# Attention probabilities turned in 32x32 blocks on VectorE and moved between partition quadrants by DMA, in a two-layer encoder trunk

## The chip, the cores and the metric

The kernel runs on one core of a Trainium2 chip. The metric is device time in microseconds, the median of several executions. A core has a matrix engine (TensorE, PE in the profile, with its weight loads as PEld), VectorE (DVE), ScalarE (ACT), GpSimd (POOL), and SyncE (SP), whose queue here issues nearly all DMAs. The on-chip memory SBUF has 128 partitions; a quadrant is 32 of them. Matmuls write to PSUM, which is divided into banks.

## The reference

Two identical layers over a sequence of 256 positions with 1024 channels, in float32. Each layer is a half-step SwiGLU block, a mixer and another half-step SwiGLU block. The mixer is where the change is:

```python
h = rms_norm(x, norm_mix[l])
proj = h @ w_in[l]                       # q, k, v, u, g: 512 columns each
q, k, v, u, g = jnp.split(proj, splits, axis=-1)
a = dilated_attention(partial_rotary(heads(q)), partial_rotary(heads(k)), heads(v))   # 8 heads x 64
sg = gelu(u) * (w_s @ layer_norm(gelu(g)) + b_s)                                      # 4 groups x 128
mixed = concatenate([rms_norm(a, out_norm_attn[l]), rms_norm(sg, out_norm_sgu[l])])
x = x + mixed @ w_out[l]
```

The three dilated softmaxes of the attention, merged by their denominators, are computed as one softmax over 256 keys with an additive bias table. The output is the final RMSNorm of x.

## The kernel before, in words

Positions lie on partitions: `NT = 2` tiles of 128. Every product with a weight matrix is made of three matmuls of 512 columns: weights and activations are split into a high part (`hi`, type fp32r) and a remainder (`lo`), and `multiply` (L150) adds hi x hi, hi x lo and lo x hi for each block of 128 rows `k` and each position tile `t`. One call of `multiply` uses one *unit* of the weight stream, 4 blocks of 128 x 512, so 24 matmuls. Before its matmuls, `run_ahead` (L139) writes down the next work of the stream: the load of a unit up to five ahead (`load_unit`, one DMA of 1 MB on SP into one of 3 `raw` buffers, L119) and the split of the unit two ahead (`split_unit`: on ScalarE the high part `whi`, L133; on VectorE the remainder `wlo`, L134; 3 buffers each). A load waits for the split that frees its `raw` buffer. The argument `among` of `multiply` names functions that are called ahead of block `j`, so that other work is written between the matmuls.

The order in which the program is written is not the order in each engine's queue. A planner takes the written order as priority and, with its own estimates of how long each instruction takes, puts on each engine the first instruction that it believes ready. The queues are fixed when the program is built, and each engine then works through its own in order.

The mixer (`mixer`, L511) goes through the units q, k, v, g, u and then four units of `w_out`. The attention is done in two groups of four heads (`a` = 0, 1):

- `scores(a, t)` makes q times k in PSUM, and a VectorE instruction (L571) adds the bias table and takes the row maximum; `softmax(a, t)` takes exponentials on ScalarE (L580) and scales by the reciprocal sum on VectorE (L583). The result `pr[a]` has queries on partitions. `attend(0)` and `attend(1)` are written into the two g units.
- `turn_probs(a)` turns `pr[a]` so that keys lie on partitions: 16 transposes of 128x128 on TensorE (L596) into PSUM tiles `pt`, copied to `prT[a]` half by VectorE (L598), half by ScalarE (L600). It is written into the first u unit for group 0 and at the start of the second for group 1.
- `values(a)` multiplies `prT[a]` by v (tile `pav`, L627, 16 matmuls of 256 columns) and evacuates to `aT` (L632 on ScalarE, L633 on VectorE) and to its squares `sq` (L635). It is written ahead of blocks 1 and 3 of the second u unit.
- `normalise` takes Gelu and layer norm of g to `vv` (L649 to L658). `gate` multiplies `vv` by the spatial weights (tile `mixed`, L690) and by `uu`, the Gelu of u (L678), to `sg`; `turn_sg` transposes that to `sgT`.
- The output projection takes `aT` (accumulators `oa`, two of them, `d` = 0, 1) and then `sgT` (accumulators `os`). `square_sums` (tile `ss`, L673) and `inverse_root` give the norm's factor, and `add` (L705) adds an accumulator to x with it.

Accumulators come from a PSUM pool of four banks, two for each of `g`, `u`, `oa` and `os`; a bank is free again when its last reader is done: `normalise` for g, `uu` for u, `add` for `oa`. Another pool of four banks holds `sc`, `pt`, `pav`, `mixed` and `ss`. Tiles with the same tag (`h0` to `h5`) share one SBUF buffer in turn.

Of the kernel before, what the change touches and what calls it, by code (L numbers as in the profile page):

```python
# [10 lines left out]
F32 = mybir.dt.float32  # L11
F32R = mybir.dt.float32r
BF16 = mybir.dt.bfloat16
AF = mybir.ActivationFunctionType
ALU = mybir.AluOpType
PSUM = bass.MemoryType.PSUM

P = 128
D = 1024
S = 256  # L20
NT = S // P
DEPTH = 2
H = 8
DH = 64
DA = 512
# [62 lines left out]
def trunk_kernel(ctx: ExitStack, tc: tile.TileContext, ws, x, cxt, rows, sgw, ident, bias, rot, out):  # L88
    nc = tc.nc
# [3 lines left out]
    big = ctx.enter_context(tc.tile_pool(name="big", bufs=1))  # L93
# [3 lines left out]
    ps_sc = ctx.enter_context(tc.tile_pool(name="ps_sc", bufs=4, space=PSUM))  # L97
# [52 lines left out]
    def multiply(acc, lhs, start, stop, among={}):  # L150


        i = done["used"]
        done["used"] += 1
        run_ahead(i + 1)
        hi, lo = splits.pop(i)
        ks = UNITS[i][2]
        for j, k in enumerate(ks):
            if j in among:
                among[j]()  # L160
            xh, xl = lhs(k)
            wh, wl = hi[:, j * W:(j + 1) * W], lo[:, j * W:(j + 1) * W]
            for t in range(NT):
                s = slice(t * P, (t + 1) * P)
                nc.tensor.matmul(acc[t], xh[:, s], wh, start=start and j == 0, stop=False)  # L165
                nc.tensor.matmul(acc[t], xh[:, s], wl, start=False, stop=False)  # L166
                nc.tensor.matmul(acc[t], xl[:, s], wh, start=False, stop=stop and j == len(ks) - 1)  # L167
# [35 lines left out]
    def accumulators(name, pool=None, tag="acc"):  # L203
        return [(pool or ps_acc).tile([P, W], F32, tag=tag, name=f"{name}{t}") for t in range(NT)]
# [54 lines left out]
    def inverse_root(ssq, n):  # L259

        v = small.tile([P, 3, NT], F32, tag="root", name="root")
        if ssq.shape[2] == 2:
            nc.gpsimd.tensor_tensor(v[:, 0], ssq[:, :, 0], ssq[:, :, 1], op=ALU.add)
            src = v[:, 0]
        else:
            src = ssq[:, :, 0]
        nc.gpsimd.tensor_scalar(v[:, 1], src, 1.0 / n, EPS, op0=ALU.mult, op1=ALU.add)
        nc.gpsimd.tensor_tensor(v[:, 2], v[:, 1], half.to_broadcast([P, NT]), op=ALU.pow)
        return v[:, 2]
# [241 lines left out]
    def mixer(l, st, nxt):  # L511
# [28 lines left out]


        pr = [big.tile([P, NT, 4, S], F32, tag=f"h{2 + a}", name="pr") for a in range(2)]
        prT = [big.tile([P, 4, 2, S], F32, tag="h4", name="prT")]
        mx = small.tile([P, NT, 2, H], F32, tag="mx", name="mx")
        sm = small.tile([P, NT, 2, H], F32, tag="sm", name="sm")

# [39 lines left out]
        def attend(a):  # L586
            for t in range(NT):
                scores(a, t)
                softmax(a, t)

        def turn_probs(a):
            for h in range(4):
                pt = ps_sc.tile([P, 2, S], F32, tag="sc", name="pt")
                for kt in range(2):
                    for t in range(NT):
                        nc.tensor.transpose(pt[:, kt, t * P:(t + 1) * P], pr[a][:, t, h, kt * P:(kt + 1) * P], id_sb)  # L596
                if h % 2:
                    nc.vector.tensor_copy(prT[a][:, h], pt)  # L598
                else:
                    nc.scalar.activation(prT[a][:, h], pt, AF.Copy)  # L600

        multiply(accs[0], st.lhs, False, True)
        rotate(0, r8)
# [8 lines left out]

        acc_g = accumulators("g")
        multiply(acc_g, st.lhs, True, False, {2: lambda: attend(0)})
        multiply(acc_g, st.lhs, False, True, {1: lambda: attend(1)})


        aT = big.tile([P, 2, 4, S], F32R, tag="h1", name="aT")
# [2 lines left out]
        def values(a):  # L621
            bank = ps_sc.tile([P, 2, S], F32, tag="sc", name="pav")
            for p in range(2):
                for kt in range(2):
                    for j in range(2):
                        h = 2 * p + j
                        nc.tensor.matmul(bank[j * DH:(j + 1) * DH, p], vs[:, kt, (4 * a + h) * DH:(4 * a + h + 1) * DH],  # L627
                                         prT[a][:, h, kt], start=kt == 0, stop=kt == 1)
            for p in range(2):
                k = 2 * a + p  # L630
                g = col(l, 24 + k)
                nc.scalar.activation(aT[:, 0, k], bank[:, p], AF.Copy, scale=g)  # L632
                nc.vector.scalar_tensor_tensor(aT[:, 1, k], bank[:, p], g, f32(aT[:, 0, k]),  # L633
                                               op0=ALU.mult, op1=ALU.subtract)
            nc.scalar.activation(sq[:, 2 * a:2 * a + 2], bank, AF.Square)  # L635


        acc = accumulators("u")
        prT.append(big.tile([P, 4, 2, S], F32, tag="h0", name="prT"))
        multiply(acc, st.lhs, True, False, {1: lambda: turn_probs(0)})  # L640
        vv = big.tile([P, NT, W], F32, tag="vv", name="vv")

        def normalise():

            vn = [act.tile([P, W], F32, tag="s", name="vn") for _ in range(NT)]
            st6 = small.tile([P, NT, 6], F32, tag="st6", name="st6")
            mv = small.tile([P, NT, 2], F32, tag="mv", name="mv")
            for t in range(NT):
                tc.keep_in_program_order(nc.scalar.activation(vn[t], acc_g[t], AF.Gelu, scale=r[:, t:t + 1]))  # L649
                nc.vector.bn_stats(st6[:, t], vn[t])  # L650
                nc.vector.bn_aggr(mv[:, t], st6[:, t])
            rs = small.tile([P, 2, NT], F32, tag="rs", name="rs")
            nc.gpsimd.tensor_scalar(rs[:, 0], mv[:, :, 1], 1.0, EPS, op0=ALU.mult, op1=ALU.add)
            nc.gpsimd.tensor_tensor(rs[:, 1], rs[:, 0], half.to_broadcast([P, NT]), op=ALU.pow)
            for t in range(NT):
                nc.vector.scalar_tensor_tensor(vn[t], vn[t], mv[:, t, 0:1], ln_sb[:, l, 0],
                                               op0=ALU.subtract, op1=ALU.mult)
                nc.vector.scalar_tensor_tensor(vv[:, t], vn[t], rs[:, 1, t:t + 1], ln_sb[:, l, 1],  # L658
                                               op0=ALU.mult, op1=ALU.add)

        def values_and_gate():
            values(0)
            normalise()

        multiply(acc, st.lhs, False, True, {0: lambda: turn_probs(1), 1: values_and_gate, 3: lambda: values(1)})
        nc.vector.tensor_tensor(sq[:, :2], sq[:, :2], sq[:, 2:], op=ALU.add)
        nc.vector.tensor_tensor(sq[:, 0], sq[:, 0], sq[:, 1], op=ALU.add)
        ssq_a = small.tile([P, NT, 1], F32, tag="ssq_a", name="ssq_a")

        def square_sums():  # L670
            bank = ps_sc.tile([P, NT, 1], F32, tag="sc", name="ss")
            for t in range(NT):
                nc.tensor.matmul(bank[:, t], sq[:, 0, t * P:(t + 1) * P], ones, start=True, stop=True)  # L673
            nc.vector.tensor_copy(ssq_a, bank)
# [4 lines left out]


        sg = big.tile([P, NT, W], F32, tag="sg", name="sg")
        sgT = big.tile([P, 2, 4, S], F32R, tag="h2", name="sgT")
        ssq_s = small.tile([P, NT, 1], F32, tag="ssq_s", name="ssq_s")

        def gate():
            for g0 in (0, 2):
                bank = ps_sc.tile([P, 2, NT, P], F32, tag="sc", name="mixed")
                for g in range(2):
                    s = slice((g0 + g) * P, (g0 + g + 1) * P)
                    nc.tensor.matmul(bank[:, g], sgw_sb[:, l, g0 + g, :], vv[:, :, s], start=True, stop=True)  # L690
                for g in range(2):
                    s = slice((g0 + g) * P, (g0 + g + 1) * P)
                    nc.vector.scalar_tensor_tensor(sg[:, :, s], bank[:, g], col(l, 32 + g0 + g), uu[:, :, s],
                                                   op0=ALU.add, op1=ALU.mult)
            for t in range(NT):
                square_sum(ssq_s[:, t], sg[:, t])
# [5 lines left out]
        def add(acc, d, rt):  # L702
            for t in range(NT):
                xs = x_sb[:, t, d * W:(d + 1) * W]
                nc.vector.scalar_tensor_tensor(xs, acc[t], rt[:, t:t + 1], xs, op0=ALU.mult, op1=ALU.add)  # L705
# [4 lines left out]
        def a_lhs(k):  # L710
            return aT[:, 0, k], aT[:, 1, k]

        for d in (0, 1):
            acc = accumulators("oa")
            multiply(acc, a_lhs, True, True, {1: gate, 3: square_sums} if d == 0 else {0: turn_sg})
            if d == 0:
                r_a = inverse_root(ssq_a, DA)
            add(acc, d, r_a)
        r_s = inverse_root(ssq_s, DG)
        new = nxt()  # L720
        for d in (0, 1):
# [97 lines left out]
```

## Time and profile before

| what | value |
|---|---|
| median of 3 runs | 920.57 us (920.27 to 920.67) |
| profiled execution | 922.07 us, span 920.3 us |
| busy: PE / PEld / DVE / ACT / POOL | 912.4 / 750.2 / 751.1 / 466.3 / 21.5 us |
| granted TensorE clock | 0.999 |
| DMA | 174.14 MB, mean 189 GB/s |

The span is the time from the first to the last instruction of one profiled execution. Busy time is the time in which an engine had an instruction in work. A row of instruction groups gives line, engine and operation, output and inputs, shape and count, then busy time, mean ns of one, and idle time of the engine just before. A timeline row gives start, length, engine, line and operation, and in brackets the idle time before it and what ended it. A row of time windows gives the window, its length and then each engine's busy time in the order PE, PEld, DVE, ACT, POOL with the number of instructions, the clock, the DMA share and GB/s. The first mixer's units g to `os` lie between about 221 and 281 us, the second layer's 453 us later.

### The profile page before, as it was taken

Reading aid. Unit: us, or ns where it says so; the run is one execution under the profiler, and the core shown is the slowest. Engines: PE = TensorE matmul, PEld = TensorE weight load, DVE = VectorE, ACT = ScalarE, POOL = GpSimd, SP = SyncE. Lnnn points to the kernel's source line nnn. Section 1 sums busy time; section 2 is a strip of 40 time slices with the busy share of each in tenths; the row PEclk is TensorE's granted clock in tenths of the full one; section 3 lists DMA queues with packets and bytes.
Section 4 is the critical chain, followed back from the end, with each engine's and each line's share of the span. In section 5 each row is a group of like instructions: output and inputs, shape, how many; then the busy total and the mean of one; then the engine's idle time right before and its main releaser. Section 6 shows DMA issues by size and latency. Waiting matters only on the chain.

```text
span 920.3 us, 11062 instructions
## 1 busy us (share of the span) xinstructions
PE 912.4 (99%) x4178; PEld 750.2 (82%) x4178; DVE 751.1 (82%) x1203; ACT 466.3 (51%) x654; POOL 21.5 (2%) x48
## 2 busy tenths in 40 slices
PE   9999999999999999999999999999999999999997
PEld 6888888888778888888888888888887888888886
DVE  6698996796789699896687998966887887998854
ACT  6544544356756544434445544445467545444440
POOL 0000000000010000000000000000000100000000
PEclk9999999999999999999999999999999999999999
DMA  8765555565334645646555555455543455565351
GB/s 330 297 259 183 187 201 205 187 217 192 138 113 175 215 141 206 219 147 237 192 197 177 192 213 191 152 209 208 201 140 135 164 202 183 183 210 200 126 195 47
DMA packets 26982, 174.14 MB, mean 189 GB/s; under 512 B 3120, under 2 KB 4272, under 8 KB 6960
## 3 DMA queue, kind: packets, MB, share of 16 engines
q1 hardware_dynamic: 26496, 172.86, 52.6%
q8 instruction: 33, 0.54, 0.2%
q10 hardware_dynamic: 432, 0.56, 0.2%
q14 instruction: 21, 0.17, 0.1%
HBM read 172.36 MB, written 1.05 MB: 188 GB/s over the span
## 4 chain that ended last, share of the span: by engine, by line
PE 97%; DVE 1%; issue 1%; ACT 0%; DMA 0%; POOL 0%; POOLq 0%; DVEq 0%
PE down L165 8%; PE down L166 8%; PE down L167 8%; PE gate L166 7%; PE up L166 7%; PE up L167 7%; PE gate L167 7%; PE up L165 7%; PE gate L165 7%; PE both L166 2%; PE both L165 2%; PE both L167 2%; PE g L165 1%; PE q L167 1%; PE g L166 1%; PE os L165 1%
## 5 line engine op out<-in xcount | busy, mean ns | idle before, releaser
L134 DVE TENSOR_TENSOR wlo<-raw,whi 128x1024 fp32r<-128x1024 f32 (+2 forms) x325 | 378.4, 1201 | 105.1 <-ACT whi L133 102.8
L133 ACT ACTIVATE whi<-raw 128x1024 fp32r<-128x1024 f32 (+2 forms) x325 | 322.4, 1039 | 246.9 <-issue 100.1
L276 DVE STREAM_TRANSPOSE turned<-h 32x256 f32<-32x256 f32 (+1 forms) x384 | 158.9, 414 | 6.3
L167 PE MATMUL down<-whi,hT 128*128 128x512 f32 x340 | 132.3, 389 | 0.0
L165 PE MATMUL down<-whi,hT 128*128 128x512 f32 x340 | 132.3, 389 | 0.0
L166 PE MATMUL down<-wlo,hT 128*128 128x512 f32 x340 | 132.3, 389 | 0.0
L167 PE MATMUL gate<-whi,xTl 128*128 128x512 f32 x304 | 118.3, 389 | 0.0
L167 PE MATMUL up<-whi,xTl 128*128 128x512 f32 x304 | 118.3, 389 | 0.0
L166 PE MATMUL gate<-wlo,xTh 128*128 128x512 f32 x304 | 118.3, 389 | 0.0
L165 PE MATMUL up<-whi,xTh 128*128 128x512 f32 x304 | 118.3, 389 | 0.0
L166 PE MATMUL up<-wlo,xTh 128*128 128x512 f32 x304 | 118.3, 389 | 0.0
L165 PE MATMUL gate<-whi,xTh 128*128 128x512 f32 x304 | 118.1, 389 | 0.0
L167 PEld LDWEIGHTS down<-whi,hT 128*128 128x128 f32 x340 | 63.8, 188 | 13.3
L165 PEld LDWEIGHTS down<-whi,hT 128*128 128x128 f32 x340 | 63.8, 188 | 13.3
L166 PEld LDWEIGHTS down<-wlo,hT 128*128 128x128 f32 x340 | 63.8, 188 | 13.2
L279 ACT ACTIVATE hT<-turned 128x512 fp32r<-128x512 f32 x44 | 26.8, 626 | 80.2 <-DVE turned L276 80.2
L165 PEld LDWEIGHTS gate<-whi,xTh 128*128 128x128 f32 x304 | 57.1, 188 | 11.9
L165 PEld LDWEIGHTS up<-whi,xTh 128*128 128x128 f32 x304 | 57.1, 188 | 11.9
L166 PEld LDWEIGHTS up<-wlo,xTh 128*128 128x128 f32 x304 | 57.1, 188 | 11.9
L166 PEld LDWEIGHTS gate<-wlo,xTh 128*128 128x128 f32 x304 | 57.1, 188 | 11.9
L167 PEld LDWEIGHTS up<-whi,xTl 128*128 128x128 f32 x304 | 57.1, 188 | 11.8
L167 PEld LDWEIGHTS gate<-whi,xTl 128*128 128x128 f32 x304 | 57.0, 188 | 11.8
(172 smaller groups left out, 1064.7 us busy)
## 6 DMA issues: line engine op xcount, KB each, us to landing
raw<-in_ws SPq DMA_DIRECT2D x154, 1024.0 KB, 4.8
raw<-in_ws SPq DMA_DIRECT2D x8, 512.0 KB, 3.2
raw<-in_ws SPq DMA_DIRECT2D x7, 256.0 KB, 5.5
x_sb<-in_x SPq DMA_DIRECT2D x1, 1024.0 KB, 10.8
ln_sb<-in_rows SPq DMA_DIRECT2D x1, 1024.0 KB, 7.4
out<-y SPq DMA_DIRECT2D x2, 320.0 KB, 2.5
xt_sb<-in_cxt SPq DMA_DIRECT2D x1, 512.0 KB, 7.9
sgw_sb<-in_sgw SPq DMA_DIRECT2D x1, 512.0 KB, 6.5
```

What stands on the lines that cost most here:

```text
L133: nc.scalar.activation(hi[:, s], raw[:, s], AF.Copy)
L134: nc.vector.tensor_tensor(lo[:, s], raw[:, s], f32(hi[:, s]), op=ALU.subtract)
L165: nc.tensor.matmul(acc[t], xh[:, s], wh, start=start and j == 0, stop=False)
L166: nc.tensor.matmul(acc[t], xh[:, s], wl, start=False, stop=False)
L167: nc.tensor.matmul(acc[t], xl[:, s], wh, start=False, stop=stop and j == len(ks) - 1)
L276: nc.vector.transpose(to[32 * c:32 * c + 32, :, :, b, :], frm[32 * b:32 * b + 32, :, :, c, :])
L279: nc.scalar.activation(dst_hi, src, AF.Copy)
```

## The change

`turn_probs(a)` no longer uses TensorE or PSUM. Two VectorE transposes (one per position tile) turn each 32x32 block of `pr[a]` within its own quadrant and write to `tmp`; then 16 DMAs on SP move each quadrant's blocks (32 partitions x 2 KB) to the quadrant they belong to, in `dst`, which takes over the buffer of `pr[a]`. `values` reads `dst` through a pattern of runs of 32 elements. The calls are written at other places: `turn_probs(0)` right after the first g unit, `turn_probs(1)` after the second, `normalise` ahead of the second u unit, `values(0)` ahead of the last block of that unit, and `values(1)` with `gate` ahead of block 2 of the first `oa` unit. Both `oa` accumulators are opened together; the square sums, `turn_sg` and the first `add` are written into the second `oa` unit. `sgT` moves from buffer `h2` to `h5`.

```diff
-        prT = [big.tile([P, 4, 2, S], F32, tag="h4", name="prT")]
+        prT = []
...
         def turn_probs(a):
-            for h in range(4):
-                pt = ps_sc.tile([P, 2, S], F32, tag="sc", name="pt")
-                for kt in range(2):
-                    for t in range(NT):
-                        nc.tensor.transpose(pt[:, kt, t * P:(t + 1) * P], pr[a][:, t, h, kt * P:(kt + 1) * P], id_sb)
-                if h % 2:
-                    nc.vector.tensor_copy(prT[a][:, h], pt)
-                else:
-                    nc.scalar.activation(prT[a][:, h], pt, AF.Copy)
+            tmp = big.tile([P, 4, 16, 32], F32, tag=("h4", "h0")[a], name="prB")
+            for t in range(NT):
+                nc.vector.transpose(tmp[:, :, 8 * t:8 * t + 8].rearrange("p c q j -> p q c j"),
+                                    pr[a][:, t].rearrange("p h (k c i) -> p (h k) c i", c=4, i=32))
+            dst = big.tile([P, 4, 16, 32], F32, tag=("h2", "h3")[a], name="prT")
+            for b in range(4):
+                for c in range(4):
+                    nc.sync.dma_start(dst[32 * c:32 * c + 32, b], tmp[32 * b:32 * b + 32, c])
+            prT.append(dst)
...
         multiply(acc_g, st.lhs, True, False, {2: lambda: attend(0)})
+        turn_probs(0)
         multiply(acc_g, st.lhs, False, True, {1: lambda: attend(1)})
+        turn_probs(1)
...
-                        nc.tensor.matmul(bank[j * DH:(j + 1) * DH, p], vs[:, kt, (4 * a + h) * DH:(4 * a + h + 1) * DH],
-                                         prT[a][:, h, kt], start=kt == 0, stop=kt == 1)
+                        probs = prT[a].rearrange("p b (t q) j -> p q t b j", t=NT)[:, 2 * h + kt]
+                        nc.tensor.matmul(bank[j * DH:(j + 1) * DH, p].rearrange("p (t b j) -> p t b j", t=NT, b=4),
+                                         vs[:, kt, (4 * a + h) * DH:(4 * a + h + 1) * DH], probs,
+                                         start=kt == 0, stop=kt == 1)
...
-        prT.append(big.tile([P, 4, 2, S], F32, tag="h0", name="prT"))
-        multiply(acc, st.lhs, True, False, {1: lambda: turn_probs(0)})
+        multiply(acc, st.lhs, True, False)
...
-        def values_and_gate():
-            values(0)
-            normalise()
-
-        multiply(acc, st.lhs, False, True, {0: lambda: turn_probs(1), 1: values_and_gate, 3: lambda: values(1)})
-        nc.vector.tensor_tensor(sq[:, :2], sq[:, :2], sq[:, 2:], op=ALU.add)
-        nc.vector.tensor_tensor(sq[:, 0], sq[:, 0], sq[:, 1], op=ALU.add)
+        normalise()
+        multiply(acc, st.lhs, False, True, {3: lambda: values(0)})
...
         def square_sums():
+            nc.vector.tensor_tensor(sq[:, :2], sq[:, :2], sq[:, 2:], op=ALU.add)
+            nc.vector.tensor_tensor(sq[:, 0], sq[:, 0], sq[:, 1], op=ALU.add)
...
-        sgT = big.tile([P, 2, 4, S], F32R, tag="h2", name="sgT")
+        sgT = big.tile([P, 2, 4, S], F32R, tag="h5", name="sgT")
...
-        for d in (0, 1):
-            acc = accumulators("oa")
-            multiply(acc, a_lhs, True, True, {1: gate, 3: square_sums} if d == 0 else {0: turn_sg})
-            if d == 0:
-                r_a = inverse_root(ssq_a, DA)
-            add(acc, d, r_a)
+        def values_and_gate():
+            values(1)
+            gate()
+
+        accs = [accumulators("oa") for _ in range(2)]
+        multiply(accs[0], a_lhs, True, True, {2: values_and_gate})
+
+        def add_first():
+            add(accs[0], 0, r_a[0])
+
+        r_a = []
+
+        def root_first():
+            square_sums()
+            r_a.append(inverse_root(ssq_a, DA))
+
+        multiply(accs[1], a_lhs, True, True, {0: root_first, 1: turn_sg, 3: add_first})
+        add(accs[1], 1, r_a[0])
```

## The prediction

> **What bounds the kernel now.** I read the page's head, its busy totals and the chain that ended last first, because they say which engine the end belongs to.
>
> ```profile
> span 920.3 us, 11062 instructions
> ...
> PE 912.4 (99%) x4178; PEld 750.2 (82%) x4178; DVE 751.1 (82%) x1203; ACT 466.3 (51%) x654; POOL 21.5 (2%) x48
> ...
> PE 97%; DVE 1%; issue 1%; ACT 0%; DMA 0%; POOL 0%; POOLq 0%; DVEq 0%
> ```
>
> TensorE (PE) carries 97% of the chain: a microsecond taken off its queue is a microsecond of span, until something else is late. VectorE (DVE) is next, at 82%, and it is VectorE that gets more work here. The profiled execution took 922.07 us with a span of 920.3 us; the median of the three runs is 920.57 us. I form differences on the span and take them off the median.
>
> Next I read the chain in order of time where the transposes stand (start, length).
>
> ```profile
> 237.53 0.23 PE u L167
> 237.76 1.75 PE pt L596 x16
> 239.50 0.23 PE u L165
> ...
> 246.72 1.88 PE pav L627 x16
> ...
> 703.77 0.60 ACT sq L635
> 704.37 1.28 ACT L649
> ...
> 710.76 0.76 DVE vv L658
> 711.52 0.14 issue
> 711.65 1.96 PE mixed L690 x8
> ```
>
> Sixteen transposes cost 1.75 us between two u matmuls. There are four such groups (two head groups, two layers). In the second layer the chain leaves PE and runs through ScalarE's (ACT's) Gelu to vv: even now the side work ends just as PE needs it, so the mixer has little slack.
>
> **The change, part by part.** The groups that are removed or serve as a measure:
>
> ```profile
> L596 PE MATMUL pt<-id_sb,pr 128*128 128x128 f32 x64 | 7.6, 272 | 0.0
> L598 DVE COPY prT<-pt 128x512 f32<-128x512 f32 x8 | 5.3, 681 | 0.0
> L600 ACT ACTIVATE prT<-pt 128x512 f32<-128x512 f32 x8 | 4.2, 580 | 0.0
> L583 DVE TENSOR_TENSOR pr<-pr,sm 128x1024 f32<-128x1024 f32 x8 | 9.8, 1224 | 0.2
> L276 DVE STREAM_TRANSPOSE turned<-h 32x256 f32<-32x256 f32 x320 | 139.6, 436 | 5.2
> L276 DVE STREAM_TRANSPOSE turned<-h 32x128 f32<-32x128 f32 x64 | 19.4, 303 | 1.1
> ```
>
> *Removed.* 64 transposes: 4 x 1.75 = 7.0 us off PE, 3.5 per layer, all of it on the chain. Eight copies of 0.68 us leave VectorE and eight of 0.58 us leave ScalarE.
>
> *Added on VectorE.* Eight transposes of 128x1024. No such shape is in the trace. The two shapes that are differ by 128 elements and 133 ns, so 1.04 ns an element, and 303 - 133 = 170 ns is fixed: 170 + 1024 x 1.04 = 1.24 us if all four quadrants run side by side. The low end is that; the high end, quadrants one after another, is four times it, 4.9 us. I take 1.24, next to the 1.22 us of the 128x1024 multiply on all partitions. Net on VectorE per layer: 4 x 1.24 - 4 x 0.68 = +2.2 us.
>
> *Added on SP.* 16 copies per head group of 32 partitions x 2 KB (64 KB), 64 in all, on the queue that issues the weight loads.
>
> ```profile
> 31.25 0.43 SPq L223 DMA_DIRECT2D rot_sb<-in_rot  x1
> 31.73 0.42 SPq L223 DMA_DIRECT2D bias_sb<-in_bias  x1
> ```
> ```profile
> raw<-in_ws SPq DMA_DIRECT2D x154, 1024.0 KB, 4.8
> ...
> out<-y SPq DMA_DIRECT2D x2, 320.0 KB, 2.5
> ...
> rot_sb<-in_rot SPq DMA_DIRECT2D x1, 32.0 KB, 4.7
> ```
> ```profile
> SPq L119 <- DVE wlo L134: 74.3, 12, 13.5
> ```
>
> Issues follow at 0.48 us (31.25 to 31.73), so 16 take 7.7 us. No row shows a copy inside SBUF. For the landing I take the 2.5 us of the output store, which leaves SBUF on an idle queue; the ends are 0.4 us (the issue alone) and 4.7 us (behind loads). From the last transpose to usable probabilities it is thus 7.2 + 2.5, say 9.7 us, between 7.6 and 12. The Trainium skill, "DMA: Bandwidth & Descriptors", section "Anatomy of one DMA", gives about 2.0 us fixed plus bytes over 436 GB/s, an estimate of 2.15 us for 64 KB on a path other than this one; by it the time would be about 9.4 us. No row of this trace shows such a copy.
>
> *What waits behind them on SP.* The loads. In the 90 us around the first mixer (200 to 290) SP sat 74.3 us waiting for splits, so it has the time. A load that left at 245 us now leaves at about 254 and lands at 259 (4.8 us); its split stands at 263.2 in the trace, about 260 to 261 now. I cost this at nothing; if a landing took over 7 us the splits would slip by the rest.
>
> *The consumers are moved later* (first layer's clock).
>
> ```profile
> 236.23 0.39 PE L165 MATMUL u<-whi,xTh 128*128 128x512 f32 x1
> 236.46 0.39 PE L166 MATMUL u<-wlo,xTh 128*128 128x512 f32 x1
> ...
> 269.34 0.39 PE L165 MATMUL os<-whi,sgT 128*128 128x512 f32 x1
> ```
> ```profile
> 232.51 1.22 DVE L583 TENSOR_TENSOR pr<-pr,sm 128x1024 f32<-128x1024 f32 x1
> ...
> 240.11 1.28 DVE L598 COPY prT<-pt 128x512 f32<-128x512 f32 x2
> ...
> 241.51 1.22 DVE L583 TENSOR_TENSOR pr<-pr,sm 128x1024 f32<-128x1024 f32 x1
> ```
>
> A matmul takes 0.227 us, a unit of 24 takes 5.45. Without transposes PE is at values(0), before the last 6 of u's 48, at 236.2 + 9.5 = 245.7. Head group 0 is scaled at 233.7; its transposes end at 235 to 236 and its copies have landed by about 246. No wait, or a few tenths.
>
> values(1) is the tight one. Head group 1 is scaled at 242.7 in the trace; ahead of that VectorE gets two transposes (2.4) and loses two copies (1.3), and its own last transpose follows (1.2): about 245 to 246.5. Plus 9.7: usable at 256. PE gets to values(1) in source order at 249.0 (u ends, with values(0)'s 1.88) + 12 x 0.227 = 251.7. That is over 4 us early. The trace shows that queues are not in source order: mixed, written behind 6 oa matmuls, ran at 258.54 behind 15, when vv was there. With the first 12 matmuls of the second oa (2.7) and mixed (1.96) put ahead of it, PE arrives at 256.4, and the wait is covered. This is what I take.
>
> *What is late next.* Three things, all on VectorE and ScalarE.
>
> ```profile
> 248.65 0.47 ACT L632 ACTIVATE aT<-pav,cols_sb 128x256 fp32r<-128x256 f32 x1 [1.98 <-PE pav L627]
> ...
> 250.70 0.60 ACT L635 ACTIVATE sq<-pav 128x512 f32<-128x512 f32 x1 [0.55 <-DVE aT L633]
> ...
> 254.35 1.38 ACT L678 ACTIVATE uu<-u,root 128x512 f32<-128x512 f32 x2
> ```
> ```profile
> 263.76 0.19 POOL L267 TENSOR_SCALAR root<-ssq_a 128x2 f32<-128x2 f32 x1 [6.77 <-DVE ssq_a L674]
> 264.04 0.69 POOL L268 TENSOR_TENSOR root<-root,half 128x2 f32<-128x2 f32 x1
> ```
> ```profile
> 233.64:269.34 35.70, 35.56 (x194) 28.09 (x192) 29.42 (x53) 23.39 (x47) 4.86 (x8) 1.00 0.34 120
> ```
>
> First, the second oa's accumulators are u's banks, free only after uu (1.38 us), which on ScalarE queues behind values(0)'s evacuation (248.65 to 251.30, 2.65 us): ready at about 252, wanted at 251.7; I take 0.5 us. Second, mixed needs vv, which now starts right behind the last exponentials; I take 0.6 us. Third, os needs the first oa's banks, so add_first, so root_a, so both head groups' squares: 258.3 (values(1) ends) + 2.65 + about 1.0 for two square sums + 0.4 + 0.9 on POOL + 1.4 for add_first = 264.7 if nothing is ahead of any step, against 265.8 when PE wants it (269.3 - 3.5). But VectorE (fourth number of the row) was busy 29.4 of these 35.7 us; with +2.2, and one split (2.35) deferred past os, it is 29.3 of 32.2, 91% where it was 82%. A step then often finds an operation of 1.2 us ahead of it; three entries on VectorE, so I take 1.5 us.
>
> Waits of 0.5 + 0.6 + 1.5 = 2.6 us against 3.5 saved: 0.9 us a layer, 1.8 in all. 920.6 - 1.8 = 918.8 us.
>
> *Small items.* The values matmuls read and write 32-element runs instead of rows of 256: I take 1.88 us as now; the high end is double, 7.5 us in all. Normalise moves ahead of the second u unit, which feeds vv earlier; the table loads stay two per layer. The square sums and the sgT buffer only change place.
>
> **The rivals.**
>
> *B, nothing is late.* Copies issue faster than I take (0.33 us is the shortest issue on SP) and VectorE's idle time soaks up the rest: the whole 7.0 us, 913.6, range 912.5 to 916.5. For it: 6.3 us of VectorE idle in the row above. Against it: the second layer's chain through vv.
>
> *C, values(1) stands at its source place on PE.* The queue order is fixed ahead of the run; if the planner takes a copy for cheap, PE is at values(1) at 251.7 to 254 and stands until 256: 2.5 to 6 us of idle per layer, and everything behind it that needed values(1) starts no sooner. It decides from 3.5 us of wait on. With 4.5 to 5.5 us plus 0.5 of the other waits it gives 1.5 to 2.5 us lost per layer: 923.6 to 925.6, call it 924. This is the case on the other side.
>
> *C2, the same with a slow clock behind it.* The start shows what PE does before it has been busy:
>
> ```profile
> 8.58 0.63 PE L181 MATMUL up<-wlo,xTh 128*128 128x512 f32 x1
> 9.01 0.63 PE L182 MATMUL up<-whi,xTl 128*128 128x512 f32 x1
> ...
> 10.07 0.39 PE L182 MATMUL up<-whi,xTl 128*128 128x512 f32 x1
> 10.30 0.39 PE L180 MATMUL gate<-whi,xTh 128*128 128x512 f32 x1
> ```
>
> The matmuls start 0.43 us apart up to 9.4 us and 0.23 apart from then on. If each wait of C brings back some ten matmuls at that pace, 10 x 0.2 = 2 us more per layer: 928. The Trainium skill, "TensorE: Matmul & The Clock Gate", section "Why this matters for your kernels", says to leave no idle gaps above about 3 us between bursts, else the clock drops to half. The trace has no idle gap of PE of that length to try this on; the change of pace at the start agrees with a gate that opens with work.
>
> *D, transposes are dear.* At 4.9 us each VectorE gets 14.8 us more per layer than I took; less the 6.3 idle, and with splits then late for PE, 8 to 12 us lost per layer: 935 to 945.
>
> **How the numbers follow.** This kernel's runs agree within 0.04%, and 0.2% (1.84 us) is about what can be told from no change. Forecast 0.43, own range 916.5 to 920.8 (waits of 1.5 to 3.6 us per layer): half of it faster, half the same. B 0.14, faster. C 0.18 and C2 0.15, slower but for 0.01. D 0.06, slower. Left 0.04, no change. So faster 0.36, same 0.25, slower 0.39. The range leaves out B's best half, the upper half of C2 and D: 913.8 to 928.0. The predicted time is the likeliest case's, 918.8.
>
> **What would show it.** No pt group of L596's kind and 3.5 us less PE work per mixer: the first term. A DVE STREAM_TRANSPOSE of 128x1024 x8: 1.2 us, or D. The SP queue's 16 issues in 7 to 8 us; from the last transpose to the first pav matmul of head group 1 about 10 us. PE's idle before pav in the waits: under 1 us per layer says forecast, 3 us or more says C, with matmuls 0.43 us apart behind it C2. Idle before the second oa, mixed and os: my 0.5, 0.6 and 1.5. The prediction is wrong if the planner's order on PE keeps values(1) ahead of the second oa, or if the copies land in much less than 9 us.

## The result, and the profile after

The changed kernel takes 928.48 us (median of 4 runs, 927.73 to 929.88) against 920.53 us for the kernel before beside it: a ratio of 1.0088, 95% interval 1.0071 to 1.0106. It is 8 us slower, where 918.8 was forecast, and half a microsecond beyond the range of 913.8 to 928.0. The profiled execution took 928.1 us.

The head of its page, the busy totals, the chain, the DMA issues of the copies (count, size, median us to landing) and one group of instructions (last column: idle time of the engine just before):

```profile
span 926.3 us, 10997 instructions
...
PE 908.1 (98%) x4114; PEld 744.9 (80%) x4114; DVE 755.3 (82%) x1203; ACT 462.7 (50%) x646; POOL 21.4 (2%) x48
...
PE 92%; DVE 6%; issue 1%; POOL 1%; DMA 0%; POOLq 0%; ACT 0%; DVEq 0%
...
prT<-prB SPq DMA_DIRECT2D x64, 64.0 KB, 2.0
```
```profile
L596 DVE STREAM_TRANSPOSE prB<-pr 128x1024 f32<-128x1024 f32 x8 | 9.9, 1240 | 0.1
```

PE's busy time fell by 4.3 us, not 7.0, and VectorE (DVE) now holds 6% of the chain. To see where, I divided the span at the mixers. Time windows from the first g matmul to the first gate matmul of the next block, first of the kernel before, then of the changed one (columns: window, length, busy time of PE, PEld, DVE, ACT and POOL, clock, DMA):

```profile
221.56:281.14 59.58, 59.44 (x335) 47.55 (x334) 49.08 (x96) 40.29 (x83) 5.25 (x10) 1.00 0.36 133
674.62:734.23 59.61, 59.43 (x336) 47.56 (x334) 49.10 (x96) 40.30 (x83) 5.24 (x10) 1.00 0.37 132
```
```profile
219.96:283.37 63.41, 58.45 (x304) 45.83 (x303) 51.19 (x96) 38.48 (x79) 5.19 (x10) 0.97 0.48 158
676.85:740.26 63.41, 58.44 (x304) 45.56 (x302) 51.19 (x96) 38.47 (x79) 5.18 (x10) 0.97 0.49 158
```

Each mixer is 3.8 us longer, 7.6 in all; between the mixers (393.48 us in both) and behind the second (186.0) nothing changed. The two profiled executions reached the first mixer 1.6 us apart, so I compare these stretches and not the spans. 3.5 us less PE work a mixer and 3.8 us more time means that 7.3 us a mixer were lost. PE busy is 1 us less, since some of the loss is slow matmuls: the clock is 0.97 here.

What PE waited for (us in total, times, longest):

```profile
PE oa L167 <- DVE aT L639: 5.3, 2, 2.7
PE os L167 <- DVE sgT L293: 1.8, 2, 0.9
...
PE oa L165 <- ACT aT L638: 1.1, 2, 0.6
...
PE pav L632 <- DMA prT<-prB: 0.8, 1, 0.8
```

The longest is not the wait for the copies but the one behind it, for `aT`. (In the second layer PE stood 0.8 us ahead of `pav` too; the view puts that down to VectorE, so the row for the copies counts one.) PE's timeline there, in the first layer:

```profile
245.29 0.39 PE L167 MATMUL u<-whi,xTl 128*128 128x512 f32 x1
246.44 1.95 PE L632 MATMUL pav<-prT,v 128*64 128x256 f32 x16 [0.76 <-DMA prT<-prB]
248.95 0.50 PE L165 MATMUL oa<-whi,aT 128*128 128x512 f32 x1 [0.56 <-ACT aT L638]
...
249.75 0.40 PE L166 MATMUL oa<-wlo,aT 128*128 128x512 f32 x1
252.85 1.05 PE L167 MATMUL oa<-whi,aT 128*128 128x512 f32 x2 [2.70 <-DVE aT L639]
253.69 0.63 PE L165 MATMUL oa<-whi,aT 128*128 128x512 f32 x1
254.12 0.63 PE L166 MATMUL oa<-wlo,aT 128*128 128x512 f32 x1
...
255.83 0.63 PE L167 MATMUL oa<-whi,aT 128*128 128x512 f32 x1
256.25 0.50 PE L165 MATMUL oa<-whi,aT 128*128 128x512 f32 x1
256.60 0.39 PE L166 MATMUL oa<-wlo,aT 128*128 128x512 f32 x1
...
259.25 1.95 PE L632 MATMUL pav<-prT,v 128*64 128x256 f32 x16
...
271.26 0.49 PE L167 MATMUL os<-whi,sgT 128*128 128x512 f32 x1 [0.87 <-DVE sgT L293]
```

PE had 0.8 us of idle before pav, 0.6 before the first oa matmuls, did four of them, and then stood 2.7 us. Behind that, eight matmuls follow each other 0.42 to 0.43 us apart instead of 0.23: 1.6 us. Near os (idle 0.87 and the gaps on both sides of it) 1.7 us are lost. That is 0.9 + 0.6 + 2.9 + 1.6 + 1.7 = 7.7 us with the switching around each wait counted in, less 0.4 of the same kind before: the 7.3 us.

`aT` of group 0 needs its high part (ScalarE) and its remainder (VectorE). VectorE's timeline and SP's issues:

```profile
249.19 0.75 DVE L663 SCALAR_TENSOR_TENSOR vv<-vn,rs,ln_sb 128x512 f32<-128x512 f32 x1 [0.86 <-POOL rs L659]
249.86 0.75 DVE L661 SCALAR_TENSOR_TENSOR vn<-vn,mv,ln_sb 128x512 f32<-128x512 f32 x1
250.52 1.22 DVE L134 TENSOR_TENSOR wlo<-raw,whi 128x1024 fp32r<-128x1024 f32 x1
251.65 0.74 DVE L663 SCALAR_TENSOR_TENSOR vv<-vn,rs,ln_sb 128x512 f32<-128x512 f32 x1
252.32 0.48 DVE L639 SCALAR_TENSOR_TENSOR aT<-pav,cols_sb,aT 128x256 fp32r<-128x256 f32 x1
```
```profile
234.79 10.10 SPq L601 DMA_DIRECT2D prT<-prB  x16
244.98 0.53 SPq L119 DMA_DIRECT2D raw<-in_ws  x1
245.98 11.78 SPq L601 DMA_DIRECT2D prT<-prB  x16
```

The remainder stands in VectorE's queue behind the layer norm. `pav` was done and ScalarE's high part written at 248.9 (248.42 + 0.47), but VectorE then still had three steps of the layer norm and a split to do, until 252.3. And the 16 copies of group 0 take SP 10.10 us to issue, 0.63 us each; PE starts pav 1.55 us after the last (244.89 to 246.44). For group 1 the issue ends at 257.76, and PE starts its pav at 259.25, 1.49 us later: without a recorded wait, but, judged by group 0, hardly before its data arrives.

So two things met here: copies that come late, and an order on VectorE that puts `aT` late. The experiments take them one at a time, as far as the planner lets them: where an edit changes what it counts on, it changes PE's order too. Stretch below means the time from the first g matmul to the first gate matmul, first layer first; times are medians, and ratios are to the kernel before (920.3 to 920.4 us beside each).

### The profile page after: what moved, and what is told of

It reads as the page before. It is cut to its first block, busy times and chain, and to the rows that moved or that the text cites. A ratio compares the mean times of both kernels' runs of the same rounds, so it can differ in the third digit from the quotient of the medians.

```text
span 926.3 us, 10997 instructions
## 1 busy us (share of the span) xinstructions
PE 908.1 (98%) x4114; PEld 744.9 (80%) x4114; DVE 755.3 (82%) x1203; ACT 462.7 (50%) x646; POOL 21.4 (2%) x48
## 4 chain that ended last, share of the span: by engine, by line
PE 92%; DVE 6%; issue 1%; POOL 1%; DMA 0%; POOLq 0%; ACT 0%; DVEq 0%
PE down L167 8%; PE down L166 8%; PE down L165 8%; PE gate L167 7%; PE up L167 7%; PE gate L166 7%; PE up L166 7%; PE up L165 7%; PE gate L165 7%; DVE wlo L134 2%; PE both L167 2%; PE both L165 2%; PE both L166 2%; DVE prB L596 1%; DVE pr L583 1%
```

## The experiments

**e1: the new places with the old turning.** `turn_probs` keeps its new call places and uses TensorE again.

```diff
-            tmp = big.tile([P, 4, 16, 32], F32, tag=("h4", "h0")[a], name="prB")
-            ... (two VectorE transposes, 16 copies)
+            dst = big.tile([P, 4, 2, S], F32, tag=("h4", "h0")[a], name="prT")
+            ... (16 TensorE transposes, 4 copies from PSUM, as before)
```

> The kernel after, with every call where the change puts it, but the probabilities turned as before (16 transposes on TensorE, copies on VectorE and ScalarE). Theory A (late copies and the queue orders written for them cost 7.5 us a layer): neither is left, TensorE has its 3.5 us a layer back, so about 920 to 922 us. Theory B (moving the calls is what costs, whatever turns the probabilities): waits of 3 us or more a layer stay on PE, 926 us or more.

Measured: 923.08 us, ratio 1.0029 [1.0018, 1.0040]; stretch 60.87 and 60.89, 1.3 us over before. The rearrangement alone costs, but only a third of the 3.8 us by which a mixer grew.

**e2: the copies left out.** `values` reads `tmp`, so blocks are not moved between quadrants and the output is not the reference's.

```diff
-            dst = big.tile([P, 4, 16, 32], F32, tag=("h2", "h3")[a], name="prT")
-            ... (the 16 copies)
-            prT.append(dst)
+            prT.append(tmp)
```

> The kernel after without its 64 copies: the second product reads the blocks where VectorE wrote them, so the output is wrong and the time is that of the change with copies that cost nothing. Theory A (copies): 913.5 to 917 us, most of the 7 us of TensorE work is seen as gain, and the 2.7 us wait for the remainder of aT is under 0.7 us. Theory C (VectorE has too much work with 8 transposes of 1.24 us): waits of 2 us or more a layer stay, 919 us or more.

Measured: 916.17 us, ratio 0.9953 [0.9938, 0.9968]; stretch 57.43 and 57.48. What the copies cost is thus 6.0 us a mixer (63.41 - 57.43), with the order that PE has without them. VectorE's remainder of `aT` and PE around it in e2:

```profile
252.19 0.48 DVE L635 SCALAR_TENSOR_TENSOR aT<-pav,cols_sb,aT 128x256 fp32r<-128x256 f32 x1
```
```profile
244.13 1.95 PE L628 MATMUL pav<-prB,v 128*64 128x256 f32 x16
...
248.50 1.95 PE L628 MATMUL pav<-prB,v 128*64 128x256 f32 x16
...
252.33 0.70 PE L688 MATMUL mixed<-vv,sgw_sb 128*128 128x256 f32 x2 [0.76 <-DVE vv L659]
```

The remainder is no earlier on VectorE here (252.19 against 252.32). But PE had work until 251.6: six u matmuls behind group 0's values, group 1's values and four more oa matmuls lie ahead of it, where in the changed kernel all of u lay ahead of group 0's values and group 1's copies were not there until about 259. Late copies did not only make PE wait for pav; they took away what covered the layer norm.

**e3: the order on VectorE.** `normalise` is written behind `values(0)`, as it was before.

```diff
-        normalise()
-        multiply(acc, st.lhs, False, True, {3: lambda: values(0)})
+        def values_first():
+            values(0)
+            normalise()
+
+        multiply(acc, st.lhs, False, True, {3: values_first})
```

> One call moved: normalise is written behind values(0) instead of ahead of the second u unit, so that on VectorE the remainder of aT comes ahead of the layer norm of g. Theory A in the form that the order of VectorE's queue makes the wait (aT behind vn, vv and a split): the 2.7 us wait falls below 1 us, the matmuls behind it keep their 0.23 us pace, 3 to 4.5 us a layer come back, 920 to 923 us. If instead the copies' landing sets the end, the wait only moves: 926 us or more.

Measured: 929.60 us, ratio 1.0097 [1.0080, 1.0114]. The wait for the remainder of `aT` is gone from PE's waits, and another has its place:

```profile
PE pav L632 <- DMA prT<-prB: 6.1, 2, 3.2
```

SP finished the issues of group 1 at 258.96 in this run, and pav started at 260.46, again 1.50 us later. (This profiled execution took 933.13 us, 3.5 more than the median, so its waits may be longer than in the others.) The order alone is not the cause: with it mended, PE runs into the copies.

**e4: no idle gap.** 20 matmuls whose result is not used are written where PE stood.

```diff
+        def keep_busy():
+            sink = ps_sc.tile([P, S], F32, tag="sc", name="sink")
+            for i in range(20):
+                nc.tensor.matmul(sink, aT[:, 0, 0, :P], aT[:, 0, 0], start=True, stop=True)
+
-        multiply(accs[0], a_lhs, True, True, {2: values_and_gate})
+        multiply(accs[0], a_lhs, True, True, {0: keep_busy, 2: values_and_gate})
```

> The kernel after with 20 more matmuls of 256 columns on TensorE (their result is not used), placed between the first values and the first oa matmuls, where PE stood idle for 2.9 us; the other queues keep their order. If the idle time slows the clock (matmuls 0.43 us apart for some 3.7 us after it), the pace stays at 0.23 us and 1 to 1.7 us a layer come back in spite of the added work: 925 to 926.5 us. If the slow pace has another cause, it stays, and the time is 928 us or more.

Measured: 927.46 us, ratio 1.0074 [1.0059, 1.0089], between the two expectations; no matmul 0.43 apart is left in the mixers, so the idle time brought the slow clock. But of the 3 us that it took in two layers only some 1.0 came back (928.48 - 927.46; the intervals of the two ratios overlap). The first mixer is 0.6 us shorter (62.82), the second is not (63.56), where PE stood 1.8 us ahead of group 0's values instead of 0.8. PE now arrives earlier at group 1's pav and waits there for the copies, 0.5 us in the first layer (put down to the issue) and 1.3 in the second; of the waits for copies in both:

```profile
PE pav L632 <- DMA prT<-prB: 2.0, 2, 1.3
```

**e5: two queues.** Every second copy is issued by ScalarE.

```diff
-                    nc.sync.dma_start(dst[32 * c:32 * c + 32, b], tmp[32 * b:32 * b + 32, c])
+                    (nc.scalar if c % 2 else nc.sync).dma_start(dst[32 * c:32 * c + 32, b], tmp[32 * b:32 * b + 32, c])
```

> Every second copy between the quadrants (odd c) is issued by ScalarE instead of SyncE, so that each queue issues 8 of a group instead of 16; nothing else changes. Theory 'the issue of the copies on one queue sets the end' (0.63 us each, 10 to 12 us a group in the changed kernel): a group is issued in about 5 to 6 us, the probabilities stand about 5 us earlier, and the waits of pav and of aT behind them fall by most of what the copies cost; the mixer stretch (first g matmul to first gate matmul) goes from 63.4 us to 59 to 61 us, the time to 919 to 924 us. Rival 'the transfers themselves are slow' (each copy's 2 us landing, or the transfer engines): the copies land as late as before, stretch 63 us or more, time 927 to 930 us. Second rival 'ScalarE pays': 8 issues a group at 0.5 us or more delay ScalarE's exponentials and evictions, and the waits move to ScalarE's results (u, aT); time 924 to 928 us with waits of PE on ScalarE.

Measured: 934.32 us, ratio 1.0155 [1.0141, 1.0169], outside all three expectations. ScalarE's timeline:

```profile
229.64 1.99 ACT L133 ACTIVATE whi<-raw 128x1024 fp32r<-128x1024 f32 x2
234.41 5.38 ACTq L601 DMA_DIRECT2D prT<-prB  x8
239.84 0.51 ACT L580 ACTIVATE pr<-pr,mx 128x256 f32<-128x256 f32 x1 [8.20 <-DMA prT<-prB]
```

The issue of a group did halve (eight in 5.38 us). But a DMA issue waits in its engine's queue like any instruction: ScalarE stood from 231.6 until the transposes were done at 234.4, issued until 239.8, and only then began group 1's exponentials (237.16 in the changed kernel). Group 1's copies were issued from 248.4 instead of 246.0. The planner had put the first of group 1's values ahead of all oa matmuls, and PE stood there for 7.9 us. "ScalarE pays" was right in kind, but the time is 6 us above the upper end that I gave it, and part of that is the planner's order.

**e6: the new turning at the old places.**

```diff
+        multiply(acc, st.lhs, True, False, {1: lambda: turn_probs(0)})
...
+        multiply(acc, st.lhs, False, True, {0: lambda: turn_probs(1), 1: values_and_gate, 3: lambda: values(1)})
... (VectorE transposes and 16 copies as in the changed kernel, the rest as before)
```

> The turning through VectorE and the 16 copies a group is kept, but each step stands where it stood in the kernel before: the turning of group 0 within the second u product, that of group 1 within the first gate product, values(0) and then the layer norm behind it, values(1) at the end of that product, and the tail (gate, square sums, root) in the old order. With e1 (old turning, new places: 923.1 us) this gives the fourth corner of turning times places. Theory 'the copies need a lead, and the new places exist to give it': about 10 us of copies now fall between the turning and its use, group 1 above all; 930 to 940 us, with waits of pav on the copies of 3 us and more a layer. Rival 'the rearranged places cost, and the turning is cheap': without the +1.3 us a layer of the places the time falls to 922 to 926 us. If the two effects only add: 928.5 - 2.6 = 926 us.

Measured: 941.53 us, ratio 1.0228 [1.0214, 1.0242], the first theory, 1.5 us above its range; PE waited for the copies 7.4 us ahead of group 0's values in each layer.

```profile
PE pav L628 <- DMA prT<-prB: 17.6, 3, 7.5
```

The four corners, as difference to before: new places alone +2.7 us, new turning alone +21, both +8. The places cost with the old turning and save 13 us with the new one: they give the copies a lead, and it is not enough.

**e9 and e10: the number of issues.** e9 makes the 16 copies of a group four of 128 partitions (256 KB each) that don't cross quadrants, so that the blocks lie wrong; e10 splits each copy in two.

```diff
+                nc.sync.dma_start(dst[:, b], tmp[:, b])                                   # e9, for each b
...
+                    for half in (0, 1):                                                   # e10, for each b and c
+                        nc.sync.dma_start(to[:, 8 * half:8 * half + 8], frm[:, 8 * half:8 * half + 8])
```

> As the changed kernel, but the 16 copies of a group (32 partitions, 64 KB each) are made four copies of all 128 partitions (256 KB each), straight from block c to the same block without crossing the quadrants: the same bytes on the same queue in a quarter of the issues. (The blocks then lie in the wrong quadrants; only the time is read.) Theory 'the number of issues on SyncE's queue sets when the probabilities are there' (0.63 us each): a group is issued in 2.5 us instead of 10, no wait of PE on copies and none of aT beyond that of the kernel without copies (e2: 916.2 us); 916 to 919 us. Rival 'the bytes set it': four copies of 256 KB land as late as sixteen of 64 KB, 925 to 929 us, with aT and pav late as in the changed kernel.

> As the changed kernel, but each copy is split into two of half the elements (32 partitions, 32 KB): the same bytes, from and to the same places, in 32 issues a group instead of 16. Theory 'the number of issues sets it': a group takes about 20 us to issue, both groups 40 us, so the second group is ready some 18 to 20 us later than in the changed kernel; the planner has its 24 oa matmuls to cover 10 of them, so the mixer stretch grows by 8 to 18 us a layer: 944 to 965 us, with waits of pav on the copies. Rival 'the bytes set it': 927 to 931 us, as the changed kernel.

Measured: e9 918.76 us, ratio 0.9983 [0.9974, 0.9992]; e10 969.95 us, 1.0540 [1.0525, 1.0555]. SP's issues of the first layer, e9 and then e10 (the view ends at 275 us, where 29 of e10's second 32 had been issued), and PE's waits of e9:

```profile
234.91 2.47 SPq L600 DMA_DIRECT2D prT<-prB  x4
...
246.04 2.42 SPq L600 DMA_DIRECT2D prT<-prB  x4
```
```profile
234.94 20.23 SPq L603 DMA_DIRECT2D prT<-prB  x32
255.26 0.53 SPq L119 DMA_DIRECT2D raw<-in_ws  x1
255.96 19.21 SPq L603 DMA_DIRECT2D prT<-prB  x29
```
```profile
PE oa L167 <- DVE aT L638: 1.8, 2, 1.0
PE pav L631 <- DMA prT<-prB: 1.7, 2, 0.9
```

An issue takes 0.62, 0.63 and 0.63 us for 256, 64 and 32 KB: the same bytes cost 2.5, 10.1 or 20.2 us by their number alone. With 12 issues fewer a group, 9.7 us of the 12.3 that the copies cost (928.48 - 916.17) came back. Both waits are still there, at 0.9 us a layer each instead of none as I expected, with the remainder of `aT` as late on VectorE as before (252.43). With 16 more a group, the first mixer grew by 20.7 us (63.41 to 84.14), as much as the 32 more issues of a layer take (32 x 0.63 = 20.2), and the time is 5 us over my upper end; pav starts 1.4 us after group 0's last issue there as well (255.17 to 256.55). e10 has the order of PE's groups of the changed kernel; e2 and e9 have another, since the planner counts in fewer copies. So the loss by more issues is shown at a fixed order, and the gain by fewer with the order that goes with it. e9's copies also stay within their quadrants, so it alone does not tell the number from the path; e10 keeps the path and the bytes. The issue count on one queue sets when the copies are there. The Trainium skill's page "DMA: Bandwidth & Descriptors", section "Rules for kernel authors", advises to join many small transfers into one large one; e9 agrees.

**e11: GpSimd as the second queue.** As e5, with `nc.gpsimd` in place of `nc.scalar`.

> Every second copy between the quadrants (odd c) is issued by GpSimd instead of SyncE. In e5 ScalarE's eight issues a group stood 8 us in front of its exponentials, since its queue waits in order for the transposes; GpSimd has no exponentials, only the maxima's negation, the root of the layer norm and the like. Theory 'one queue's issue sets it, and GpSimd is free to share it': 918 to 923 us. Rival 'GpSimd pays as ScalarE did': its small steps (mx, rs), for which ScalarE and VectorE wait, stand behind its copies, and the softmax of group 1 or the layer norm comes late: 926 to 935 us, with waits on POOL's mx or rs or on the copies.

Measured: 934.73 us, ratio 1.0159 [1.0144, 1.0173]: the second rival again. GpSimd's timeline:

```profile
235.40 4.14 POOL L601 DMA_DIRECT2D prT<-prB  x8 [7.96 <-PE g L167]
239.57 1.16 POOL L577 TENSOR_SCALAR mx<-mx 128x4 f32<-128x4 f32 x2
...
252.88 4.02 POOL L601 DMA_DIRECT2D prT<-prB  x8 [8.58 <-DVE prB L596]
```

Its eight copies stand ahead of the two `mx` that group 1's exponentials wait for; these ran at 239.6. The planner had put the layer norm ahead of group 1's scaling on VectorE, the last transpose began at 250.99 instead of 244.60, group 1's copies left at 252.9, and pav waited 4.8 us. The Trainium skill's page "DMA: Bandwidth & Descriptors", section "Issuing engines are not separate DMA queues", says that issuing on several engines saves only the sequencers' issue time, which it calls usually small beside the DMA itself. Here the issue was the large part (10.1 us beside 2.0 us of landing) and was halved; it was lost again because the new queue had work of its own to do, and because the order on the other engines moved with it.

**e7, e8 and e12: one group each way.** Group 0 has a lead: nothing needs it until the end of u. Group 1 has none. In e7 group 0 is turned by VectorE and copied at its early place, group 1 by TensorE at its old place, and the tail is the old one.

```diff
+            if a == 0:
+                ... (two VectorE transposes, 16 copies on SP)
+                return
+            prT.append(big.tile([P, 4, 2, S], F32, tag="h0", name="prT"))
+            ... (16 TensorE transposes as before)
...
-        turn_probs(1)
...
+        multiply(acc, st.lhs, False, True, {0: lambda: turn_probs(1), 1: normalise, 2: lambda: values(0), 3: lambda: values(1)})
```

e8 does the same, but shares group 0's copies with ScalarE and calls `values(0)` ahead of `normalise`. e12 has the places of e7 and turns both groups by TensorE.

> Group 0 is turned by VectorE with its 16 copies on SyncE, called early as in the changed kernel; group 1 is turned by TensorE as before, called at its old place in the gate product, and the tail stands in the old order; values(0) is called behind the third chunk of the gate product. TensorE loses 16 of its 32 transposes a layer (1.75 us). Theory 'the lateness of the copies costs, and one group alone has time to arrive': no wait of pav on copies, stretch 57.9 to 59.2 us against 59.6 us before, time 917.5 to 920.5 us, at or just below the kernel before. Rival 'every rearrangement of the planner's order costs about 1 us a layer, copies or not' (as e1 showed +1.3): 920.5 to 924 us. Rival 'the copies of one group still hold aT back': 922 to 926 us with pav waiting on the copies.

> As e7, with the copies of group 0 shared out between the queues of SyncE and ScalarE, and values(0) called where the kernel before called it, ahead of the layer norm. Theory 'issue on one queue is the cost': the copies are there 4 to 5 us earlier than with one queue, nothing waits for them, stretch 57.9 to 59 us, time 917.5 to 919.5 us. Rival 'ScalarE pays for its 8 issues': waits on ScalarE's evictions (u, prT, aT) of 1 to 2 us a layer, 920 to 924 us. If one queue was enough for one group, e7 and e8 differ by less than 1 us.

> The call places of e7 (group 0 turned straight after its softmax, group 1 in the gate product, values(0) behind the third chunk, the tail in the old order), but both groups are turned by TensorE as in the kernel before. Theory 'e7 gains by the transposes that TensorE no longer does' (16 a layer, 1.75 us, 3.5 us in all): this kernel is 2 to 4 us slower than e7, 920 to 922 us, mixer stretch about 60 us. Rival 'e7 gains by its places': this kernel is as fast as e7, 917.5 to 918.7 us.

Measured: e7 918.06 us, ratio 0.9976 [0.9967, 0.9985]; e8 923.00, 1.0029 [1.0017, 1.0040]; e12 921.32, 1.0011 [1.0002, 1.0020]. Windows of the mixers of e7, and its waits of PE:

```profile
219.68:278.17 58.49, 57.59 (x319) 45.93 (x318) 50.10 (x96) 39.58 (x81) 5.14 (x10) 1.00 0.44 153
671.67:730.18 58.51, 57.63 (x319) 45.93 (x318) 50.11 (x96) 39.58 (x81) 5.14 (x10) 1.00 0.44 154
```
```profile
PE pt L608 <- DVE sm L582: 0.9, 2, 0.5
PE ss L691 <- DVE sq L685: 0.8, 2, 0.4
```

e7 beats both kernels, by 2.4 us over the one before. PE waits for no copy, and the clock is whole. Against e12, which differs in the turning of group 0 alone (and in the order that the planner makes of it), it gains 3.3 us of the 3.5 that 32 transposes cost. e8, with its copies issued in half the time, is 4.9 us slower than e7: one queue was enough for one group, and ScalarE's eight issues cost it `prT` and exponentials (pav waits 0.9 us a layer for ScalarE's copy, pt 1.3 us in one layer for exponentials). Since e8 also has another place for `values(0)`, not all of the 4.9 us need be the queue's.

## Why the prediction was wrong, step by step

- *Removed: 7.0 us of TensorE.* Right: no transposes of `pr` are left, and e7 against e12 measured 3.3 us for half of them.
- *VectorE's transposes at 1.24 us.* Right: 1240 ns mean. Rival D falls. The values matmuls through runs of 32 elements cost nothing either (16 in 1.95 us in the timeline, before and after).
- *Copies, 9.7 us from the last transpose to usable.* Too small, by the term "Issues follow at 0.48 us". The landing was shorter than taken (2.0 us, and PE started 1.5 us after the last issue), but 16 issues took 10.10 us, and 11.78 for group 1, with 1.9 us of waits on SP for a load in flight and for earlier copies. Group 0's last transpose ends at 234.7 and pav starts at 246.44: 11.7 us. For group 1 (245.8 to 259.25) it was 13.4. Counted from the first g matmul, group 1's values began at 39.3 us, where 34.4 had been worked out (256 less 221.56): 3.7 of these 4.9 us are the copies, the rest transposes that ended later than taken. The issue cost came from two loads of small tables from HBM; nothing in the trace of before showed one between quadrants, and I took no upper end for it.
- *values(0): "No wait, or a few tenths".* PE was there at 245.7 and waited 0.8. That the time agrees is chance: this mixer had begun 1.6 us earlier than in the profile before, and the planner had put all 48 u matmuls ahead of values(0), not 42, so that none was left to cover what follows. What I did not list under "what is late next", and so put at nothing, is the evacuation of values(0). Its remainder stands on VectorE behind the layer norm, which the change moved ahead, and PE had nothing else to do but four matmuls. With the pace behind it this is 5 us of the 7.3 a mixer (0.6 + 2.9 + 1.6).
- *values(1), "the tight one".* The planner did move it, behind 24 oa matmuls rather than 12 and mixed, and no wait is recorded. So C, with its wait at values(1), did not occur. But it was no safe cover: in e3 and e4 PE came there 0.5 to 3.2 us early, and it waited.
- *Waits of 0.5, 0.6 and 1.5 us.* For u's banks and for mixed: nothing. For os: 1.7, close in size, though the wait that ends last is `sgT`, behind two splits on VectorE.
- *C2's slow clock* came, and its 928 is nearly the time measured, by luck: it had the wait at values(1), and the measured one is for `aT`. By e4, what the clock added to the end is about 1.0 us, not 4, since the copies stand right behind it. The Trainium skill's page "TensorE: Matmul & The Clock Gate", section "Why this matters for your kernels", advises against idle gaps of PE above about 3 us; here a stand of 2.7 us after two shorter ones was enough.
- *The loads, "at nothing".* Held for PE: between the mixers and behind them the times are unchanged.

Two steps failed. The term "Issues follow at 0.48 us" was too small: 0.63 us on this path, so that 9.7 us from the last transpose became 11.7 and 13.4. It came from a row of another kind of DMA. And the wait behind values(0) was put at nothing: 2.9 us of standing for the remainder of `aT`, with slow matmuls behind it. I had checked the consumers of each buffer that changed, but not the order of what stands around them on VectorE once they change. Each hides behind the other. With the order mended and the copies as they are, nothing is gained (e3, 929.6); with quick copies and `aT` as late on VectorE, PE has other work in the order that the planner then makes, and the loss is gone (e9, 918.8). What copies of just 9.7 us would have cost in the changed kernel's order, no run shows. The sign that I gave for the forecast, under 1 us of idle per layer before pav, came true with 0.8 us while the time went the other way: the idle time stood behind pav, where I had named no sign.

## What to carry to other kernels

Count the DMAs of a step and multiply by the issue time of their queue: 16 copies of 64 KB were 10 us of one queue by their number alone, and moving half of them to an engine with other work delayed that work by the wait as well as by the issues. Replacing work of the bounding engine by a path with a long latency paid here only where the consumer had that much lead: one group of two had it (e7, 0.9976), both together did not (1.0088). When a wait that is named last is mended and the time stays, look for the second one that was hidden just behind it, and for the work that used to cover both.

## What the runs showed of the hardware

- A copy inside SBUF took 0.62 to 0.63 us to issue on SP, at 32 and 64 KB between quadrants and at 256 KB within them, where the table loads in the kernel before followed each other at 0.48 us; eight copies of 64 KB took 5.38 us on ScalarE and 4.14 us on GpSimd.
- The matmuls ran at 0.42 to 0.43 us for 3.4 us (252.85 to 256.25) after PE had stood for 2.7 us, and at once at 0.23 when unused matmuls filled that gap (e4).
- A transpose of 32x32 blocks over all 128 partitions took 1.24 us for 1024 elements a partition, about as long as the 1.22 us of a multiply of the same shape.
